# Low halves of split weights: a subtraction, or a negated copy and an accumulating DMA

## Chip, core and metric

One core of a Trainium2 chip runs the whole program. The metric is the time of one execution on the device in microseconds (us); the time of a kernel is the median of several runs. Profiles are of one execution each.

## What is computed

A trunk of two encoder layers on x of 512 tokens by 1024 features, all in float32. Cut to the lines that carry the large matrix products:

```python
def reference(x, ...):
    for l in range(DEPTH):                                   # DEPTH = 2
        h = x @ w_in[l]                                      # inside hybrid_mixer: 1024 -> 1824
        y_a = s5_mixer(...)                                  # state space scan and gated unit, 256 channels
        y_b = gla_mixer(...)                                 # gated linear attention, 4 heads, 256 channels
        y_c = swa_mixer(...)                                 # windowed attention, 8 heads, 512 channels
        mix = concatenate([y_a, y_b, y_c]) @ w_out[l]        # 1024 -> 1024
        x = layer_norm(DEEPNORM_ALPHA * x + mix, ln1_g[l], ln1_b[l])
        hid = square(relu(x @ w_ff1[l]))                     # 1024 -> 4096
        x = layer_norm(DEEPNORM_ALPHA * x + hid @ w_ff2[l], ln2_g[l], ln2_b[l])
    return x
```

## The kernel before

Every large product runs on TensorE (PE) in three passes. Both factors are split in a high half, the value copied to the type float32r, and a low half, the value minus that copy; `mm3` (lines 248 to 250) multiplies low by high, high by low and high by high into the same PSUM bank. The tensor `WA` holds six slots of such weight pairs, 128 x 2 x 1024 each, and the slots go round.

`wunit` (line 232) makes one unit, 128 rows by up to 1024 columns. SyncE (SP) issues the load of the float32 weights from HBM into one of two `raw` buffers (line 240), ScalarE (ACT) copies it to the high half (line 217, `copyA`), and VectorE (DVE) or GpSimd (POOL) subtracts the high half from raw to make the low half (line 244). Which engine subtracts is read from the table `CFG`: a letter for each of the four units of a matrix, G for POOL and V for DVE.

In each layer the input projection runs as four projections in the order g1, g0, g2, g3 (`proj`, 4 units each; g0 has units of 576 columns, the others of 1024), each over four token tiles of 128 with 24 matmuls a tile. The first twelve of a tile read x's feature tiles 0 to 3 and the units 0 and 1, the last twelve the feature tiles 4 to 7 and the units 2 and 3; in the trace the former read XTP and the latter XTQ in layer 0, XTQ and XTR in layer 1. Between the projections lie the S5 tables, states, scan and output, the GLA gates, scores, states and output, and four windowed softmax attention blocks. Then come w_out in two halves of 512 columns (keys wo0 and wo1, 4 units each), layer norm, the first four hidden tiles of w_ff1 (key f1e, 4 units), the rest of w_ff1 and w_ff2. The units of the rest of w_ff1 and of w_ff2 give `wunit` no engine and subtract on DVE; pairs of hidden tiles in seven products have a split of their own (line 1055).

With six slots, the third and fourth unit of a projection take the slots of the first two units of an earlier one. For g0, g2 and g3 this is the projection just before, so their copies wait until its last token tile has read those units.

The order on each engine's queue isn't the program's: a planner simulates the program with its own costs for instructions and DMAs as it writes the queues, and takes what is ready first. Each queue then runs in order on the chip and waits at semaphores. GpSimd's queue also holds the products of the GLA gates and keys, the softmax scaling of one head of each group of four (line 954), half of the table products of layer 0 and some additions of layer norm (line 226).

Of the kernel before, what the change touches and what calls it, by code (L numbers as in the profile page):

```python
# [13 lines left out]
AF = mybir.ActivationFunctionType  # L14
ALU = mybir.AluOpType
AX = mybir.AxisListType
MUL, ADD, SUB, MAX, MIN = ALU.mult, ALU.add, ALU.subtract, ALU.max, ALU.min

L = 512
D = 1024  # L20
# [7 lines left out]
CFG = {  # L28
    "ln": ["SA", "SA", "SA", "SA"],
    "ln2": ["A", "GV", "VG", "SS"],  # L30
    "lnl": ["AS", "SA", "S", "SS"],
    "f1e": "GGGV",
    "wo0": "GGGG",
    "wo1": "VVVV",
    "norm": "GVAV",
    "pt": "VAAV",
    "st": [12, 4],
# [15 lines left out]
    "gg": "GGGV",  # L53
    "sq": [["V", "A"], ["A", "A"]],
    "sa": "VVVV",
    "g0": "GGGG",
    "g1": "VVVG",
    "g2": "GVVV",
    "g3": "VVVV",
}  # L60
CONST_COLS = {"ident": 128, "tri_f": 128, "tri_b": 128, "tri_sf": 128, "tri_sb": 128,
              "rope_c": 64, "rope_s": 64, "pat": 16}
# [2 lines left out]
def trunk(tc, I, out, dbg=None):  # L65
    nc = tc.nc
# [134 lines left out]
        return t  # L201

    def yk(k):
        """(tile, index) of y's k-th row tile"""
        return (M.Ya, k) if k < 2 else (M.Yb, k - 2) if k < 4 else (M.Yc, k - 4)

    def bc(ap, axis, n):
# [5 lines left out]
    def act(o_, i_, f, **kw):  # L213
        S.activation(out=o_, in_=i_, func=f, **kw)  # L214
# [13 lines left out]
    state["pair"] = 0  # L228

    def E(k, i):  # L230
        return {"G": G, "V": V, "A": S}[CFG[k][i]]

    def wunit(src, eng=None, cuts=1):
        n = src.shape[-1]
        raw = rawp.tile([128, 1024], F32, tag="raw", name="raw")
        i = state["pair"] % 6
        state["pair"] += 1
        for j in range(cuts):
            c = slice(n * j // cuts, n * (j + 1) // cuts)
            nc.sync.dma_start(raw[:, c], src[:, c])  # L240
        for j in range(cuts):
            c = slice(n * j // cuts, n * (j + 1) // cuts)
            copyA(WA[:, i, 0, c], raw[:, c])
            (eng or V).tensor_tensor(WA[:, i, 1, c], raw[:, c], WAf[:, i, 0, c], op=SUB)  # L244
        return WA[:, i, 0, :n], WA[:, i, 1, :n]

    def mm3(ps, a, b, first, last):
# [35 lines left out]
        V.tensor_tensor(M.XS[i][:, :, 1], Tr[i], M.XSf[i][:, :, 0], op=SUB)  # L283

    def rsqrt(y, v, t):
        """y = v ** -0.5"""
        yi = y.bitcast(I32)
        V.tensor_scalar(yi, v.bitcast(I32), 1, None, op0=ALU.logical_shift_right)
        V.tensor_scalar(yi, yi, -1.0, float(0x5f3759df), op0=MUL, op1=ADD)
        for _ in range(3):  # L290
            V.tensor_tensor(t, y, y, op=MUL)
            V.scalar_tensor_tensor(t, t, -0.5, v, op0=MUL, op1=MUL)
            V.scalar_tensor_tensor(y, t, 1.5, y, op0=ADD, op1=MUL)
# [3 lines left out]
        nc.sync.dma_start(M.lnb, I[f"ln{which}_b"][l:l + 1, :].to_broadcast([128, 1024]))  # L297

    def layer_norm(tt, engs, nst=2, done=None):
        """engs: the engine that scales each of the tile's column parts"""  # L300
        x = XR[:, tt]
        s = LNS[:, tt]
        w = 1024 // nst
        for h in range(nst):
            V.bn_stats(s[:, 6 * h:6 * h + 6], x[:, w * h:w * h + w])
        mean, var, rstd, nmr, tmp = [s[:, i:i + 1] for i in (24, 25, 0, 1, 2)]
        V.bn_aggr(s[:, 24:26], s[:, 0:6 * nst].rearrange("p (a b) -> p a b", a=nst))
        n = 1024 // len(engs)
        parts = [(slice(n * h, n * h + n), e) for h, e in enumerate(engs)]
        early = [c for c, e in parts if e in "SA"]  # L310

        def centre():
            if early:
                c = early.pop(0)
                V.scalar_tensor_tensor(x[:, c], x[:, c], mean, M.lng[:, c], op0=SUB, op1=MUL)

        act(tmp, var, AF.Sqrt, bias=eps_c)
        V.tensor_scalar(var, var, EPS, None, op0=ADD)
        centre()
        V.reciprocal(nmr, tmp)  # L320
        centre()
        V.tensor_tensor(tmp, nmr, nmr, op=MUL)
        centre()
        V.scalar_tensor_tensor(tmp, tmp, -0.5, var, op0=MUL, op1=MUL)
        while early:
            centre()
        V.scalar_tensor_tensor(rstd, tmp, 1.5, nmr, op0=ADD, op1=MUL)
        if any(e not in "SA" for e in engs):
            V.scalar_tensor_tensor(nmr, mean, -1.0, rstd, op0=MUL, op1=MUL)
        for c, e in parts:  # L330
            if e == "S":
                V.scalar_tensor_tensor(x[:, c], x[:, c], rstd, M.lnb[:, c], op0=MUL, op1=ADD)
            elif e == "A":
                act(x[:, c], x[:, c], AF.Copy, scale=rstd)
                tt_(G, x[:, c], x[:, c], M.lnb[:, c], ADD)
            else:
                act(x[:, c], x[:, c], AF.Identity, scale=rstd, bias=nmr)
                tt_(G if e == "G" else V, x[:, c], x[:, c], M.lng[:, c], MUL)
                tt_(G if e == "G" and done else V, x[:, c], x[:, c], M.lnb[:, c], ADD)
            if done:  # L340
                done(c)
# [517 lines left out]
        copyA(M.gv[:, tt], ps[:, 256:512])  # L859

    def rope(x, n, tt):
        """x: [128, n, 64], its first 16 dims rotated in place"""
        c = bc(rope_c[:, tt], 1, n)
        s = bc(rope_s[:, tt].rearrange("p (a b) -> p a b", a=2), 1, n)
        t1 = RT[:, 0, 0:16 * n].rearrange("p (n d) -> p n d", n=n)
        t2 = RT[:, 1, 0:16 * n].rearrange("p (n a b) -> p n a b", n=n, a=2)
        r = x[:, :, 0:16]
        V.tensor_tensor(t1, r, c, op=MUL)
        V.tensor_tensor(t2, r.rearrange("p n (a b) -> p n a b", a=2)[:, :, ::-1], s, op=MUL)
        V.tensor_tensor(r, t1, t2.rearrange("p n a b -> p n (a b)"), op=ADD)  # L870
# [158 lines left out]
                xt(k, slice(t0, t1)), k == 0, k == 7)  # L1029

    def ff1_pair(l, i):
        """hidden row tiles i and i + 1 in seven products of halves (Winograd's form)"""
        q = state["st"] % 2
        state["st"] += 1
        r1, r2 = MA[:, 2048 * q:2048 * q + 1024], MA[:, 2048 * q + 1024:2048 * q + 2048]
        nc.sync.dma_start(r1, I["w_ff1"][l, i])
        nc.sync.dma_start(r2, I["w_ff1"][l, i + 1])
        s12 = rawp.tile([128, 1024], F32, tag="raw", name="s12")
        s1, s2, s4 = s12[:, 0:512], s12[:, 512:1024], MA[:, 6144:6656]
        tt_(E("sa", 0), s1, r2[:, 0:512], r2[:, 512:1024], ADD)  # L1040
        tt_(E("sa", 1), s2, s1, r1[:, 0:512], SUB)
        tt_(E("sa", 2), s4, r1[:, 512:1024], s2, SUB)
        tt_(E("sa", 3), r2[:, 0:512], r1[:, 0:512], r2[:, 0:512], SUB)

        def unit(src, half=None):
            if half != 1:
                u = state["pair"] % 6
                state["pair"] += 1
                if half == 0:
                    state["s4"] = u  # L1050
            else:
                u = state["s4"]
            c = slice(0, 1024) if half is None else slice(512 * half, 512 * half + 512)
            copyA(WA[:, u, 0, c], src)
            V.tensor_tensor(WA[:, u, 1, c], src, WAf[:, u, 0, c], op=SUB)  # L1055
            return WA[:, u, 0, c], WA[:, u, 1, c]

        wa, w12, w3 = unit(r1), unit(s12), unit(r2)
        w4 = unit(s4, q)
        pa, pb_ = psA("f1s"), psB("f1s")  # L1060
        pc = (psC, psE)[q]("f1s")
        p1, p5, p6, p7 = [pa[:, j // 2, 256 * (j % 2):256 * (j % 2) + 256] for j in range(4)]
        p2, p3, p4 = pb_[:, 0:256], pb_[:, 256:512], pc[:, 0:256]
        m1, u2, u3 = [MA[:, 4096 + 1024 * q + 256 * j:4352 + 1024 * q + 256 * j] for j in range(3)]
        r0, r1_ = ft_r[i % 2], ft_r[(i + 1) % 2]
        c12, c21, c22 = r0[:, 256:512], r1_[:, 0:256], r1_[:, 256:512]
        X1, X2 = M.XT
        T1, T2, T3, T4 = M.XS

        def prod(ps, w, c0, x):  # L1070
            for k in range(4):
                c = slice(c0 + 128 * k, c0 + 128 * k + 128)
                mm3(ps, (w[0][:, c], w[1][:, c]), (x[:, k, 0, 0:256], x[:, k, 1, 0:256]), k == 0, k == 3)

        prod(p1, wa, 0, X1)
        copyA(m1, p1)
        prod(p5, w12, 0, T1)
        prod(p6, w12, 512, T2)
        tt_(V, u2, m1, p6, ADD)
        tt_(V, c12, u2, p5, ADD)  # L1080
        prod(p7, w3, 0, T3)
        tt_(V, u3, u2, p7, ADD)
        tt_(V, c22, u3, p5, ADD)
        prod(p2, wa, 512, X2)
        tt_(V, r0[:, 0:256], m1, p2, ADD)
        prod(p3, w4, 0, X2[:, :, :, 256:512])
        tt_(V, c12, c12, p3, ADD)
        act(r0, r0, AF.Relu)
        ff_act(None, i)
        prod(p4, w3, 512, T4)  # L1090
        tt_(V, c21, u3, p4, SUB)
        act(r1_, r1_, AF.Relu)
        ff_act(None, i + 1)
# [40 lines left out]
                return  # L1134
            n = n and n - 1

# [1 line left out]
    nc.scalar.dma_start(cst["ident"], I["cst"][:, 0:128])  # L1138
    copyA(KON[:, 2:3], KON[:, 0:1])
    state["l"] = 0  # L1140
# [195 lines left out]
```

## Time and profile before

| | |
|---|---|
| median of 3 runs | 1257.71 us (1256.9 to 1258.25) |
| span of the profiled execution | 1254.5 us, 3.2 us below the median; no other time of it is recorded |
| PE busy | 1181.2 us, 94% of the span |
| PE weight loads busy | 982.9 us, 78% |
| DVE busy | 920.8 us, 73% |
| ACT busy | 551.0 us, 44% |
| POOL busy | 165.3 us, 13% |
| DMA moved | 119.60 MB, 95 GB/s on average |

The span runs from the first to the last instruction of the program. Busy time is the union of an engine's instructions; PE's matmuls overlap their weight loads. Of the span's 40 slices PE is busy less than 90% in eleven of the first and middle ones, where the mixers run, and nearly always in the feed-forward parts. POOL works in the first ten slices and again in the middle.

### The profile page before, as it was taken

Reading aid. Unit: us, or ns where it says so; the run is one execution under the profiler, and the core shown is the slowest. Engines: PE = TensorE matmul, PEld = TensorE weight load, DVE = VectorE, ACT = ScalarE, POOL = GpSimd, SP = SyncE. Lnnn points to the kernel's source line nnn. Section 1 sums busy time; section 2 is a strip of 40 time slices with the busy share of each in tenths; the row PEclk is TensorE's granted clock in tenths of the full one; section 3 lists DMA queues with packets and bytes.
Section 4 is the critical chain, followed back from the end, with each engine's and each line's share of the span. In section 5 each row is a group of like instructions: output and inputs, shape, how many; then the busy total and the mean of one; then the engine's idle time right before and its main releaser. Section 6 shows DMA issues by size and latency. Waiting matters only on the chain.

```text
span 1254.5 us, 18971 instructions
## 1 busy us (share of the span) xinstructions
PE 1181.2 (94%) x7400; PEld 982.9 (78%) x7400; DVE 920.8 (73%) x1918; ACT 551.0 (44%) x929; POOL 165.3 (13%) x123
## 2 busy tenths in 40 slices
PE   6798878999999999999999989799999999999997
PEld 4686555578888988989987857556898898998986
DVE  8995899969877765748564399883887575764857
ACT  3253247535521633615523634662464272561640
POOL 3423262112000000000041021220300000000000
PEclk9899989999999999999999999899999999999999
DMA  5440441113344422412422414202143242340331
GB/s 199 108 130 10 72 138 37 52 35 100 120 158 139 154 90 68 152 51 68 152 81 79 152 34 85 102 21 81 35 165 121 67 139 64 99 153 17 102 118 67
DMA packets 49610, 119.60 MB, mean 95 GB/s; under 512 B 13296, under 2 KB 20336, under 8 KB 49520
## 3 DMA queue, kind: packets, MB, share of 16 engines
q1 hardware_dynamic: 37680, 103.53, 25.5%
q10 hardware_dynamic: 11840, 14.86, 4.8%
q8 instruction: 58, 0.95, 0.3%
q14 instruction: 32, 0.26, 0.1%
HBM read 108.44 MB, written 8.88 MB: 94 GB/s over the span
## 4 chain that ended last, share of the span: by engine, by line
PE 78%; DVE 17%; DMA 2%; ACT 2%; issue 1%; SPq 0%; POOL 0%; DVEq 0%; ACTq 0%
PE o L248 11%; PE o L249 11%; PE o L250 11%; PE f1s L248 6%; PE f1s L250 6%; PE f1s L249 6%; PE proj L250 2%; PE proj L248 2%; PE proj L249 2%; PE so L963 2%; PE pT L957 1%; PE f L249 1%; PE f L250 1%; PE f L248 1%; PE f1e L249 1%
## 5 line engine op out<-in xcount | busy, mean ns | idle before, releaser
L217 ACT ACTIVATE WA<-raw 128x1024 fp32r<-128x1024 f32 (+2 forms) x129 | 132.7, 1029 | 152.2 <-PE o L250 43.1
L244 DVE TENSOR_TENSOR WA<-raw,WA 128x1024 fp32r<-128x1024 f32 (+1 forms) x102 | 122.2, 1198 | 86.1 <-ACT WA L217 86.0
L217 ACT ACTIVATE WA<-MA 128x1024 fp32r<-128x1024 f32 (+1 forms) x72 | 64.7, 914 | 146.9 <-PE o L250 106.4
L974 DVE SCALAR_TENSOR_TENSOR XR<-XR,o 128x512 f32<-128x512 f32 (+1 forms) x81 | 52.7, 675 | 100.8 <-PE o L250 100.6
L1055 DVE TENSOR_TENSOR WA<-MA,WA 128x1024 fp32r<-128x1024 f32 (+1 forms) x72 | 74.5, 1042 | 17.4 <-ACT WA L217 17.2
L248 PE MATMUL f1s<-xs,WA 128*128 128x256 f32 x288 | 81.4, 283 | 0.0
L249 PE MATMUL f1s<-xs,WA 128*128 128x256 f32 x288 | 81.2, 282 | 0.0
L250 PE MATMUL f1s<-xs,WA 128*128 128x256 f32 x288 | 80.9, 281 | 0.0
L244 POOL TENSOR_TENSOR WA<-raw,WA 128x1024 fp32r<-128x1024 f32 (+2 forms) x27 | 61.8, 2294 | 131.4 <-ACT WA L217 123.9
L226 DVE TENSOR_TENSOR MA<-MA,f1s 128x256 f32<-128x256 f32 x120 | 49.4, 417 | 32.7 <-PE f1s L250 20.9
L226 POOL TENSOR_TENSOR XR<-XR,lt 128x512 f32<-128x512 f32 (+1 forms) x13 | 18.4, 1418 | 398.3 <-ACT XR L214 398.3
L248 PE MATMUL o<-WA,yYa 128*128 128x512 f32 (+1 forms) x162 | 64.8, 400 | 0.8 <-DVE XR L974 0.7
L249 PE MATMUL o<-WA,yQ 128*128 128x512 f32 (+1 forms) x164 | 64.5, 393 | 0.0
L248 PE MATMUL o<-WA,yQ 128*128 128x512 f32 (+1 forms) x164 | 64.4, 392 | 0.0
L248 PE MATMUL o<-WA,yYb 128*128 128x512 f32 (+1 forms) x162 | 64.2, 396 | 0.0
L249 PE MATMUL o<-WA,yYb 128*128 128x512 f32 (+1 forms) x162 | 63.9, 395 | 0.0
L249 PE MATMUL o<-WA,yP 128*128 128x512 f32 x160 | 63.9, 399 | 0.0
L250 PE MATMUL o<-WA,yYa 128*128 128x512 f32 (+1 forms) x162 | 63.8, 394 | 0.0
L249 PE MATMUL o<-WA,yYa 128*128 128x512 f32 (+1 forms) x162 | 63.8, 394 | 0.0
L248 PE MATMUL o<-WA,yP 128*128 128x512 f32 x160 | 63.8, 399 | 0.0
L250 PE MATMUL o<-WA,yYb 128*128 128x512 f32 (+1 forms) x162 | 63.7, 394 | 0.0
L250 PE MATMUL o<-WA,yQ 128*128 128x512 f32 (+1 forms) x164 | 63.7, 391 | 0.0
(532 smaller groups left out, 3577.8 us busy)
## 6 DMA issues: line engine op xcount, KB each, us to landing
raw<-in_w_ff SPq DMA_DIRECT2D x80, 512.0 KB, 3.5
MA<-in_w_ff SPq DMA_DIRECT2D x48, 512.0 KB, 3.5
raw<-in_wg SPq DMA_DIRECT2D x23, 512.0 KB, 4.0
raw<-in_w_out SPq DMA_DIRECT2D x16, 512.0 KB, 3.8
scr_out<-MA SPq DMA_DIRECT2D x8, 512.0 KB, 4.2
yc<-scr_out ACTq DMA_DIRECT2D x8, 512.0 KB, 3.4
raw<-in_wg SPq DMA_DIRECT2D x8, 288.0 KB, 3.1
hx<-scr_lag ACTq DMA_DIRECT2D x16, 128.0 KB, 6.2
```

What stands on the lines that cost most here:

```text
L217: S.activation(out=o_, in_=i_, func=AF.Copy)
L226: eng.tensor_tensor(o_, a, b, op=op)
L244: (eng or V).tensor_tensor(WA[:, i, 1, c], raw[:, c], WAf[:, i, 0, c], op=SUB)
L248: T.matmul(ps, a[1], b[0], start=first, stop=False)
L249: T.matmul(ps, a[0], b[1], start=False, stop=False)
L250: T.matmul(ps, a[0], b[0], start=False, stop=last)
L957: T.transpose(ps[:, b * 128:b * 128 + 128], P[:, h, b * 128:b * 128 + 128], ident)
L963: T.matmul(ps[64 * v:64 * v + 64, :], av[:, tt - 1 + b0 + b, 64 * v:64 * v + 64], M.pT[v][:, b].rearrange("p h q -> p (h q)"), start=(b == ...
L974: V.scalar_tensor_tensor(x, x, scale, ps, op0=MUL, op1=ADD)
L1055: V.tensor_tensor(WA[:, u, 1, c], src, WAf[:, u, 0, c], op=SUB)
```

## The change

For units whose letter in `CFG` is D, `wunit` writes the negated high half into the low half's place with a second ScalarE copy, and a DMA issued from POOL reads the same weights from HBM again and adds them to it. `raw` is then read by the first copy alone. The letters of the four projections, of both halves of w_out and of w_ff1's first four units become D, except the first two units of the first projection: its first stays on POOL and its second moves from POOL to DVE. That is 26 units in each layer, 52 in all. The other edits take docstrings and a comment out.

```diff
-    "f1e": "GGGV",
-    "wo0": "GGGG",
-    "wo1": "VVVV",
+    "f1e": "DDDD",
+    "wo0": "DDDD",
+    "wo1": "DDDD",
...
-    "g0": "GGGG",
-    "g1": "VVVG",
-    "g2": "GVVV",
-    "g3": "VVVV",
+    "g0": "GVDD",
+    "g1": "DDDD",
+    "g2": "DDDD",
+    "g3": "DDDD",
...
     def E(k, i):
-        return {"G": G, "V": V, "A": S}[CFG[k][i]]
+        return {"G": G, "V": V, "A": S, "D": "D"}[CFG[k][i]]
...
             copyA(WA[:, i, 0, c], raw[:, c])
-            (eng or V).tensor_tensor(WA[:, i, 1, c], raw[:, c], WAf[:, i, 0, c], op=SUB)
+            if eng == "D":
+                act(WA[:, i, 1, c], WAf[:, i, 0, c], AF.Copy, scale=-1.0)
+                nc.gpsimd.dma_start(WA[:, i, 1, c], src[:, c], accum_op=ADD)
+            else:
+                (eng or V).tensor_tensor(WA[:, i, 1, c], raw[:, c], WAf[:, i, 0, c], op=SUB)
         return WA[:, i, 0, :n], WA[:, i, 1, :n]
```

The keys `g0` to `g3` of `CFG` stand for the projections in the order in which they run: `g0` for wg1, `g1` for wg0, `g2` for wg2 and `g3` for wg3.

## Rows read from the trace of the kernel before

**Rows 1.** The page: span, busy time and share of engines, chain that ended last.
```profile
span 1254.5 us, 18971 instructions
PE 1181.2 (94%) x7400; PEld 982.9 (78%) x7400; DVE 920.8 (73%) x1918; ACT 551.0 (44%) x929; POOL 165.3 (13%) x123
...
PE 78%; DVE 17%; DMA 2%; ACT 2%; issue 1%; SPq 0%; POOL 0%; DVEq 0%; ACTq 0%
```

**Rows 2.** Waits of PE: waiting group, what ended it, us in total, times, longest.
```profile
PE wst L564 <- DVE MA L554: 5.0, 1, 5.0
PE qT L902 <- DVE MA L465: 4.9, 1, 4.9
PE goT L707 <- POOL ya L226: 4.6, 2, 3.7
...
PE sy L814 <- DVE GLS L288: 3.1, 2, 2.5
...
PE xt L257 <- DVE XTR L262: 2.0, 1, 2.0
PE f1e L249 <- DVE XTR L262: 1.7, 1, 1.7
```

**Rows 3.** Instructions on the tile raw: ns min/median/max, first to last start, shapes.
```profile
L244 DVE TENSOR_TENSOR WA<-raw,WA x102: 743/1224/1637, 30.5 to 1216.9; 128x1024 fp32r<-128x1024 f32 x96, 128x576 fp32r<-128x576 f32 x6
...
L244 POOL TENSOR_TENSOR WA<-raw,WA x27: 1262/2392/2837, 5.6 to 892.5; 128x1024 fp32r<-128x1024 f32 x23, 128x512 fp32r<-128x512 f32 x2, 128x576 fp32r<-128x576 f32 x2
```

**Rows 4.** Timeline, POOL and DVE, layer 0: start us, us, engine, line, operation.
```profile
21.70 4.75 POOL L244 TENSOR_TENSOR WA<-raw,WA 128x1024 fp32r<-128x1024 f32 x2 [8.28 <-ACT WA L217]
...
174.09 4.66 POOL L244 TENSOR_TENSOR WA<-raw,WA 128x1024 fp32r<-128x1024 f32 x2 [2.09 <-issue]
...
176.51 2.27 DVE L288 TENSOR_SCALAR GLS<-GLS 128x8 int32<-128x8 int32 x1
178.81 0.17 DVE L289 TENSOR_SCALAR GLS<-GLS 128x8 int32<-128x8 int32 x1
```

**Rows 5.** Timeline of DVE: five of the twenty instructions beside POOL subtractions.
```profile
5.66 1.26 DVE L432 SCALAR_TENSOR_TENSOR KD<-KD 128x16 f32<-128x16 f32 x1
...
21.87 2.27 DVE L456 TENSOR_TENSOR KD<-KD 128x16 f32<-128x16 f32 x1
...
656.39 2.36 DVE L324 SCALAR_TENSOR_TENSOR LNS<-LNS 128x1 f32<-128x1 f32 x1
...
783.22 2.35 DVE L292 SCALAR_TENSOR_TENSOR GLS<-GLS 128x8 f32<-128x8 f32 x1
...
893.26 2.10 DVE L322 TENSOR_TENSOR LNS<-LNS 128x1 f32<-128x1 f32 x1
```

**Rows 6.** Timeline, layer 0, third unit of g3: copy, subtraction, first two matmuls.
```profile
125.15 1.06 ACT L217 ACTIVATE WA<-raw 128x1024 fp32r<-128x1024 f32 x1 [2.21 <-PE proj L250]
...
128.62 1.23 DVE L244 TENSOR_TENSOR WA<-raw,WA 128x1024 fp32r<-128x1024 f32 x1
...
130.05 0.39 PE L248 MATMUL proj<-WA,XTQ 128*128 128x512 f32 x1
...
130.28 0.40 PE L249 MATMUL proj<-WA,XTQ 128*128 128x512 f32 x1
```

**Rows 7.** Timeline, layer 1, third unit of g0: copy, first matmul.
```profile
682.16 0.69 ACT L217 ACTIVATE WA<-raw 128x576 fp32r<-128x576 f32 x1 [2.39 <-PE proj L250]
...
686.12 0.30 PE L248 MATMUL proj<-WA,XTR 128*128 128x288 f32 x1
```

**Rows 8.** DMA issues of raw: count, KB each, median us to landing; minimum, median, maximum.
```profile
raw<-in_wg SPq DMA_DIRECT2D x23, 512.0 KB, 4.0
...
raw<-in_wg SPq DMA_DIRECT2D x8, 288.0 KB, 3.1
...
DMA to landing us min/median/max: 2.6/3.5/6.9
```

## The prediction

> **What bounds the kernel now.** I read the page's engine totals and the chain that ended last first [rows 1]. TensorE (PE) is busy for 1181.2 of 1254.5 us, so no more than 73.3 us of the span are free of matrix work, and the chain lies 78% on PE and 17% on VectorE (DVE). A faster DVE can gain only where PE waits for it. The second view is therefore PE's waits [rows 2]: the six listed sum to 21.3 us. They end on DVE work or on what follows directly from it, in the two stretches before w_ff1, where tables, scan, gates, softmax and layer norm run between the matmuls. From 300 us on in layer 0 and 920 us in layer 1 nothing changes but the first four w_ff1 units before it.
>
> The third view is the instructions on the raw weight tile [rows 3]: the subtractions of line 244 are 102 on DVE, median 1.22 us, and 27 on GpSimd (POOL), median 2.39. The fourth is the timeline of DVE and POOL side by side [rows 4]. While POOL ran two subtractions from 174.09 for 4.66 us, DVE's 128x8 operation at 176.51 took 2.27 us, and a like one at 178.81, after POOL had ended, 0.17. So a POOL subtraction costs DVE nearly its own length. Going through DVE's timeline I count twenty instructions that lasted at least 1 us longer than their like while POOL subtracted; the first and the last are shown, with three between them [rows 5]. Their excess adds up to 34 us.
>
> **What the change removes.** Per layer 12 units of 1024 columns and 3 of 576 leave DVE, and one (the second unit of the first projection) comes to it from POOL: 12 x 1.22 + 3 x 0.74 - 1.22 = 15.6 us (the median and, for the narrow ones, the shortest of [rows 3]), 31 us in two layers. 24 of POOL's 27 subtractions go, and with them all but some 2 us of the 34 us of stalls, since the two at the very start stay. That is 63 us of DVE time, yet each piece is worth only the PE wait behind it:
> - Tables of layer 0: PE waited 5.0 us for DVE before "wst" [rows 2]. Two POOL subtractions took 4.75 us from 21.70 [rows 4], in which the DVE chain got two short operations done, the first of them 2.27 us long [rows 5]: 4.3 us freed, and further subtractions of the same stretch free over 1 us. Gain 5.0, capped by the wait.
> - End of the projections of layer 0: "qT" waited 4.9 us [rows 2]; before it lie 4.66 us under POOL [rows 4] and two subtractions of 1.23 on DVE [rows 6]. Gain 4.9, capped.
> - Start of layer 1: a transpose of x waited 2.0 us [rows 2] after a layer norm operation of 2.36 us at 656.39 [rows 5]. Gain 2.0.
> - GLA output of layer 1: "goT" and "sy" waited 4.6 and 3.1 us in both layers [rows 2]; the operation at 783.22 took 2.35 us [rows 5] where 0.16 is usual. Gain 2.2.
> - First w_ff1 matmuls of layer 1: 1.7 us of waiting [rows 2] behind the 2.10 us at 893.26 [rows 5]. Gain 1.7.
>
> Together 15.8 us. What is late next at each place is PE itself. For the subtractions outside these places, on POOL or DVE, I count nothing: the DVE time that they free lies beside PE work.
>
> **What the change adds.** Each of the 52 units gets a second ScalarE (ACT) copy like the first, 1.06 us for 1024 columns [rows 6] and 0.69 for 576 [rows 7], 52 us in all, and a DMA issued from POOL that reads the weight again and adds it into WA. ACT holds 2% of the chain [rows 1], so nearly all of its 52 us lie beside other work; the bounds are 0 and, if the eight w_out copies that fall among the softmax's exponentials, four in each layer, each delay one by a whole copy, 8.5 us. I take 1.5, near the lower end, because of that 2%.
>
> The accumulating DMA is not in this trace. Its lower bound is the plain load of as many bytes; its upper bound the slowest such load, 6.9 us, plus one POOL operation of the size that it replaces, 2.3 us, for making the request: 9.2. In between: 512 KB land in 4.0 us and 288 KB in 3.1 [rows 8], so 224 KB cost 0.9 us, 512 KB 2.1 and the fixed part is 1.9. If the bytes pass twice (source and old contents) this gives 1.9 + 2 x 2.1 = 6.1 us, and 4.3 for 288 KB. I take this estimate; the lower end is the fastest plain median, 4.0.
>
> So the low half comes 1.06 + 6.1 = 7.2 us after the high half, where DVE's subtraction took 1.2. Most units have more room, their slots being free long before they are read. Not so the third and fourth unit of a projection, since their slot comes free only near the end of the projection before. In layer 0 the copy starts at 125.15, the subtraction at 128.62, and PE reads the unit first at 130.05, the thirteenth matmul of the XTQ run [rows 6]: 4.9 us of room for 2 x 1.06 + 6.1 = 8.2 us, short by 3.3. For a 576-column unit, copied at 682.16 and read at 686.12 [rows 7]: 4.0 us for 2 x 0.69 + 4.3 = 5.7, short by 1.7. There are eight such places, six wide and two narrow: 23 us if PE merely waited. But the planner that orders the queues can put the next token tile's twelve matmuls on the units already there in between: 12 x 0.23 = 2.8 us by the step from 130.05 to 130.28 [rows 6], and 1.6 for 288 columns. That leaves 6 x 0.5 + 2 x 0.1 = 3.2 us. I take 6.0: cover everywhere but at one wide place.
>
> On POOL the DMA waits for the second copy, and behind it wait the GLA products, the softmax scalings and layer norm's additions. A subtraction there waited for the first copy and held POOL for 2.3 us, so 24 places get no worse unless the request costs more than that; at the 28 places that were DVE's the added hold is up to 2.3 us, on an engine with little to do. SP's loads are not passed by anything; a raw buffer even comes free at the first copy instead of at the subtraction, which is worth nothing where the copy waits for a slot.
>
> **The sum.** 1254.5 - 15.8 + 6.0 + 1.5 = 1246.2 us of span. The median of the runs is 1257.71, 3.2 us above this span; with the same 3.2 the forecast is 1249.4, so 1249.
>
> The Trainium skill ("DMA: Bandwidth & Descriptors", section on the anatomy of one DMA) fits a GpSimd-issued DMA with 2.0 us plus bytes/436e3, an estimate of 3.2 us for 512 KB. The trace's loads of that size, issued from SP, take 4.0. By the page's figure the narrow places would have room and the wide ones would lack 0.4 us, which the reordering covers; the late units would cost next to nothing and the time would be about 1243.
>
> **Rivals.**
> 1. The low halves come late (slower). Mechanism: at the eight tight places PE stands at the first matmul of the third unit. For it speaks that the rooms of 4.9 and 4.0 us are real, against it that the planner can cover 2.8 us of each. At a DMA of 9.2 us the wide places lack 11.3 - 4.9 - 2.8 = 3.6 us even with cover, the narrow ones about as much: 29 us, so 1257.7 - 15.8 + 29 + 1.5 = 1272. It turns the sign once these places cost 14.3 us together, that is from a DMA of 7.5 us with all covers (3.2 + 8 x 1.4) and of 5.0 without any (23 - 8 x 1.1).
> 2. POOL's requests are held up by DVE (no change). They use what the subtractions used: [rows 4] show one of the two engines standing while the other works. If each request at a tight place waits for one long DVE instruction, 1.2 us as in [rows 6], 8 x 1.2 = 9.6 us are added: 1259. Against it: DVE's instructions in the tables and norms are mostly 0.2 to 0.7 us. The skill's page "SBUF — State Buffer", section "Who interferes with whom", gives this as a rule that speaks against the change: descriptor generation for a DMA issued from GpSimd is starved while DVE holds the shared port pair. No row here has such a DMA.
> 3. The freed DVE time is hidden (no change or nearly). Other POOL work, such as the table products and the softmax scalings, stays and still stalls DVE, and PE's order is rearranged; if half of the 15.8 us is lost, 1257.
> 4. More than I count: waits too small for my list close too, and all covers hold: 1257.7 - 20 = 1238.
>
> **How the numbers follow.** Forecast (1242 to 1255) 0.56; more gain (below 1242) 0.11; rivals 2 and 3 together 0.13; rival 1 0.20. The two ends of the DMA's cost give 1244 (at 4.0 us a wide place lacks 1.2, taken once) and 1272; the range 1235 to 1264 leaves out some 0.15 above and 0.04 below. 0.2% is 2.5 us, about what a measurement of this kernel can tell from no change. Faster 0.67, same 0.13, slower 0.20.
>
> **What would show each step.** Right: the 2 us operations on DVE among ones of 0.17 are gone but for the first units; line 244 on DVE falls by some 30 us, POOL by 50; "wst", "qT" and the layer norm waits shrink; ACT is busy some 52 us more. Wrong: PE waits named after WA's DMA at the third unit of projections, with sums above 10 us; landings over 7 us; POOL's requests of 2 us or more. What would overturn it altogether is a DMA that needs over 9 us from request to landing.

## The result and the profile after

| | before | after |
|---|---|---|
| median of the runs, us | 1257.9 | 1300.7 |
| profiled execution, span, us | 1254.5 | 1298.6 |
| ratio of times, 95% interval | | 1.0348 [1.0335, 1.0361] |
| PE busy, us | 1181.2 | 1196.7 |
| DVE busy, us | 920.8 | 865.2 |
| ACT busy, us | 551.0 | 597.2 |
| POOL busy, us | 165.3 | 149.6 |

The changed kernel is 3.5% slower; the prediction was 1249, faster. Its page, with the lines that answer to [rows 1] (span, busy time by engine, chain that ended last):

```profile
span 1298.6 us, 19069 instructions
...
PE 1196.7 (92%) x7400; PEld 992.2 (76%) x7400; DVE 865.2 (67%) x1890; ACT 597.2 (46%) x981; POOL 149.6 (12%) x151
...
PE 71%; DVE 12%; DMA 9%; issue 4%; ACT 2%; SPq 0%; POOL 0%; ACTq 0%; DVEq 0%; POOLq 0%
```

DVE is 56 us less busy, as intended, and its share of the chain falls from 17 to 12%. But DMA rises from 2 to 9%. POOL is only 16 us less busy, since 52 requests come where 24 subtractions go. PE does the same 7400 matmuls and is busy 15.5 us longer; with that goes a lower mean granted clock, 0.964 in the profiled run after and 0.982 in the one before (f3 and f4 below show the two together). The waits of PE, as in [rows 2] (waiting group, what ended it, us in total, times, longest):

```profile
PE proj L253 <- DMA WA<-in_wg: 17.6, 7, 5.6
PE sy L820 <- DMA yc<-scr_out: 11.0, 4, 6.4
PE wst L568 <- DVE MA L558: 9.8, 1, 9.8
PE f1e L252 <- DMA WA<-in_w_ff: 6.2, 2, 3.8
...
PE sv L743 <- DMA TAB<-scr_st: 4.5, 1, 4.5
```

Two kinds of wait are new. The first and fourth line are low halves that come late, 23.8 us. The second and the last end on DMAs that the change never touched. The third, "wst", was 5.0 us before and should have gone away; it doubled. The DMA issues of the page after (count, KB each, median us from issue to landing):

```profile
raw<-in_wg SPq DMA_DIRECT2D x23, 512.0 KB, 6.0
WA<-in_wg POOLq DMA_DIRECT2D x20, 512.0 KB, 8.5
...
WA<-in_w_out POOLq DMA_DIRECT2D x16, 512.0 KB, 6.6
...
WA<-in_w_ff POOLq DMA_DIRECT2D x8, 512.0 KB, 7.6
raw<-in_wg SPq DMA_DIRECT2D x8, 288.0 KB, 5.2
WA<-in_wg POOLq DMA_DIRECT2D x8, 288.0 KB, 8.3
```

The accumulating DMAs land in 6.6 to 8.5 us, and the plain loads beside them, 4.0 and 3.1 us in [rows 8], now take 6.0 and 5.2.

How "wst" came to double can be read from DVE's waits in the first 62 us and POOL's timeline (start us, us, engine, line, operation, idle before):

```profile
DVE CI L1167 <- DMA RT<-in_ci: 7.7, 1, 7.7
```

```profile
51.88 1.26 POOL L558 TENSOR_TENSOR MA<-lt 128x512 f32<-128x512 f32 x1
53.09 0.88 POOL L246 DMA_DIRECT2D WA<-in_wg  x1
53.70 1.35 POOL L559 TENSOR_TENSOR lt<-MB,TAB 128x512 f32<-128x512 f32 x1
54.71 1.35 POOL L560 TENSOR_TENSOR lt<-MB,TAB 128x512 f32<-128x512 f32 x1
55.71 1.19 POOL L246 DMA_DIRECT2D WA<-in_wg  x1
```

DVE, which makes the tables of layer 0, stood 7.7 us for a load of constants. Behind it the tables came later, and POOL's products of the tables with them, and the two requests for g0's third and fourth unit, ready when their second copies ended at 44.4 and 45.8, stood behind those products until 53.1 and 55.7. The subtractions they replace were on DVE and in no such queue.

### The profile page after: what moved, and what is told of

Same layout as the page of the kernel before. It is cut to its first block, busy times and chain, and to the rows that moved or that the text cites. A ratio compares the mean times of both kernels' runs of the same rounds, so it can differ in the third digit from the quotient of the medians.

```text
span 1298.6 us, 19069 instructions
## 1 busy us (share of the span) xinstructions
PE 1196.7 (92%) x7400; PEld 992.2 (76%) x7400; DVE 865.2 (67%) x1890; ACT 597.2 (46%) x981; POOL 149.6 (12%) x151
## 4 chain that ended last, share of the span: by engine, by line
PE 71%; DVE 12%; DMA 9%; issue 4%; ACT 2%; SPq 0%; POOL 0%; ACTq 0%; DVEq 0%; POOLq 0%
PE o L252 11%; PE o L253 11%; PE o L254 11%; PE f1s L252 6%; PE f1s L253 6%; PE f1s L254 6%; DMA yc<-scr_out 2%; DMA WA<-in_wg 2%; PE so L967 2%; PE f1e L252 1%; PE f1e L254 1%; PE f1e L253 1%; PE f L254 1%; PE f L253 1%; PE f L252 1%
## 5 line engine op out<-in xcount | busy, mean ns | idle before, releaser
L248 DVE TENSOR_TENSOR WA<-raw,WA 128x1024 fp32r<-128x1024 f32 x74 | 90.5, 1223 | 56.4 <-ACT WA L217 56.2
L253 PE MATMUL o<-WA,yP 128*128 128x512 f32 x160 | 63.7, 398 | 0.0
L252 PE MATMUL o<-WA,yP 128*128 128x512 f32 x160 | 63.5, 398 | 0.0
L254 PE MATMUL o<-WA,yP 128*128 128x512 f32 x160 | 63.4, 398 | 0.0
```

Of the source, the lines that this page charges most:

```text
L252: T.matmul(ps, a[1], b[0], start=first, stop=False)
L253: T.matmul(ps, a[0], b[1], start=False, stop=False)
L254: T.matmul(ps, a[0], b[0], start=False, stop=last)
```

## The experiments

Two theories stood at the start. A: the accumulating DMA is slow and shares the DMA engines with all other loads. B: the order of the queues, which the planner makes anew for each kernel, and the second ACT copies eat the gain.

### Four runs in the planner's own order

e1_plain: the DMA without its accumulation (the low half becomes the whole weight), every queue in the order of the changed kernel.

```diff
-                nc.gpsimd.dma_start(WA[:, i, 1, c], src[:, c], accum_op=ADD)
+                nc.gpsimd.dma_start(WA[:, i, 1, c], src[:, c])
```

> The changed kernel with the accumulation taken out of the DMA: it writes the weight itself into the low half, so the output lacks the correction that the low half stands for. Every engine's queue has the same order as in the changed kernel. Theory A (the accumulating DMA is slow and delays PE and other loads): its packets take 159 ns instead of 328, landings fall from a median of 7.4 us to about 5, and the time falls by 15 us or more, to 1285 or less. Theory B (the planner's new order and the second ScalarE copies cost the time, whatever the DMA takes): within 5 us of 1300.

Measured: 1275.6 us, 1.0142 [1.0119, 1.0165], as theory A had it. In the traces PE has its matmuls in the same order as in the changed kernel; there the accumulation alone costs 25 us.

e2_no_dma: no DMA at all (the low half stays minus the high half).

```diff
-                nc.gpsimd.dma_start(WA[:, i, 1, c], src[:, c], accum_op=ADD)
```

> The changed kernel without the accumulating DMAs: the low half stays the negated high half, so the correction by the low half is wrong in these 52 units. The second copies stay, the subtractions are gone. Theory A: about 1243 (1257.7 minus the 15.8 us of waits counted in the prediction, plus 1.5 for the copies), in any case below 1252. Theory B: above 1258, since the copies and a rearranged order remain.

Measured: 1261.4 us, 1.0039 [1.0028, 1.0051], as theory B had it. Without a single late low half nothing is gained over the kernel before. So the DMA alone doesn't explain the miss: 15.8 us of gain were missing here too.

e3_projections and e4_wout_ff1: the change for the projections alone, and for w_out and w_ff1 alone.

```diff
-    "f1e": "DDDD",
-    "wo0": "DDDD",
-    "wo1": "DDDD",
+    "f1e": "GGGV",
+    "wo0": "GGGG",
+    "wo1": "VVVV",
```

> Only the projections' units use the copy and the DMA (28 of 52); w_out and the first w_ff1 units subtract as before. Theory A: nearly the whole loss, 1285 to 1300, since the units without room are all here. Theory B: the loss in proportion, 28 of 52, about 1281.

```diff
-    "g0": "GVDD",
-    "g1": "DDDD",
-    "g2": "DDDD",
-    "g3": "DDDD",
+    "g0": "GGGG",
+    "g1": "VVVG",
+    "g2": "GVVV",
+    "g3": "VVVV",
```

> Only w_out and the first w_ff1 units use the copy and the DMA (24 of 52); the projections subtract as before. Theory A: no loss, 1248 to 1258, since these units have room and the layer norms and the GLA output no longer stall beside POOL. Theory B: the loss in proportion, 24 of 52, about 1278.

Measured: 1294.8 us, 1.0299 [1.0274, 1.0324], and 1265.1 us, 1.0067 [1.0047, 1.0087]. The first is what theory A had, the second lies between the two. Most of the loss belongs to the projections, where the tight units are. But every one of these kernels also has an order of its own, so no difference between them except that of e1 is clean.

### The order of before, imposed

From here on the order is held fixed. The kernel carries, for each instruction in the order of tracing, its place in the built kernel before, and ties each instruction to the one ahead of it on its engine by an edge that orders but doesn't wait (cut from the function that does it):

```diff
+    last = {}
+    for k in order:
+        if k not in base:
+            continue
+        for i in extra[k] if base[k] is None else [base[k]] + extra.get(base[k].name, []):
+            e = str(i.engine)
+            if e in last:
+                tc.add_manual_dep(i, last[e].name, mybir.DependencyInfo(
+                    mybir.DependencyClass.NoSync, mybir.DependencyReason.DATA), reason="order")
+            last[e] = i
```

`extra` holds what replaces a subtraction: the second copy right behind the first, and the request on POOL at that same point. For four w_out units, whose slots hold attention data until late, it stands where the subtraction stood. The second unit of either layer stays with POOL as before. In the traces of f1 to f9 the 7400 matmuls of PE stand in the order of before. The kernel before with its own order imposed was not run, so what imposing it does by itself is not shown.

f1_free_order_kept: the 52 subtractions are dropped, nothing replaces them.

```diff
-    "g0": "GVDD",
+    "g0": "GGDD",
...
-                act(WA[:, i, 1, c], WAf[:, i, 0, c], AF.Copy, scale=-1.0)
-                nc.gpsimd.dma_start(WA[:, i, 1, c], src[:, c], accum_op=ADD)
+                DROPS.append((nc.cur_bb.bb.instructions[-1].name, 0))
+                pass
...
-        return WA[:, i, 0, :n], WA[:, i, 1, :n]
+        return WA[:, i, 0, :n], WA[:, i, 0 if eng == "D" else 1, :n]
```

`DROPS` notes the first copy and how many instructions behind it are new, for the order; the edits below leave that line out.

> Every engine has its instructions in the order of the kernel before; the 52 subtractions are gone and nothing stands in their place: the matmuls read the high half twice, so the low halves are left out of the result. Theory A (the 15.8 us of freed VectorE waits are real, and what ate them in the run without DMA was the new order of the queues and the second copies): 1257.7 - 15.8 = 1242 us, 1238 to 1246. Theory B (the freed VectorE time is hidden, TensorE's waits only change their name): 1252 to 1257 us. Theory C (the order of before fits only its own durations, so keeping it loses something): above 1257 us.

Measured: 1233.0 us, 0.9804 [0.9780, 0.9827], below what any of the three had. Dropping the subtractions is worth 25 us, not 15.8, and the freed DVE time is not hidden. A little of the 25 is something else: f1 reads no low half in these units, so the one listed wait of PE for one of their low halves in before, 2.4 us, is gone too.

f2_copies_order_kept: f1 with the second ACT copies.

```diff
-                pass
+                act(WA[:, i, 1, c], WAf[:, i, 0, c], AF.Copy, scale=-1.0)
```

> The same order, and a second, negated ScalarE copy behind each first one, still without DMA: the low half is minus the high one, so the result lacks the weights. Theory A (ScalarE's copies lie beside other work): 1 to 3 us above the run without copies, so about 1244 us. Theory B (the copies, not the order, ate the gain of the run without DMA at 1261 us): 12 us or more above the run without copies, 1254 to 1262 us. The difference from that run of 1261 us is the price of the new order.

Measured: 1242.7 us, 0.9880 [0.9854, 0.9906]. The copies cost 10 us, which neither theory named: too much for A, too little for B. The same work in the planner's order, but for the second unit, was e2, 1261.4: that order costs some 19 us.

f3_accumulate_order_kept: f2 with the DMAs, that is the whole change in the order of before.

```diff
+                nc.gpsimd.dma_start(WA[:, i, 1, c], src[:, c], accum_op=ADD)
```

> The same order, second copies and accumulating DMAs as in the changed kernel, except that the second unit of all stays on GpSimd. Theory A (the DMA costs what it cost in the changed kernel, the order is a separate loss): plain against accumulating differed by 25 us and plain against none by 14 at the planner's own order, so 1244 + 39 = 1283 us, 1275 to 1290. Theory B (the planner's order was chosen to cover late low halves, so without it TensorE stands at every third unit): 8 places at some 5 us more, 1300 us or above. Theory C (the loss is mostly the order): below 1265 us.

Measured: 1304.4 us, 1.0355 [1.0312, 1.0399]. As theory B had it, the DMAs cost more, 62 us, in an order that doesn't make room for them. Its waits of PE (as above):

```profile
PE proj L254 <- DMA WA<-in_wg: 33.5, 13, 5.5
PE sy L821 <- DMA yc<-scr_out: 10.4, 3, 6.4
```

There are thirteen waits for low halves in the projections instead of the seven of the changed kernel: there the planner's order covered about half of them. The place of [rows 6], the third unit of layer 0's g3, in the timeline of PE and of POOL in f3:

```profile
136.84 0.39 PE L255 MATMUL proj<-WA,XTQ 128*128 128x512 f32 x1
137.07 0.40 PE L253 MATMUL proj<-WA,XTQ 128*128 128x512 f32 x1
142.39 0.80 PE L254 MATMUL proj<-WA,XTQ 128*128 128x512 f32 x1 [4.92 <-DMA WA<-in_wg]
142.99 0.63 PE L255 MATMUL proj<-WA,XTQ 128*128 128x512 f32 x1
143.41 0.63 PE L253 MATMUL proj<-WA,XTQ 128*128 128x512 f32 x1
```

```profile
134.63 0.87 POOL L247 DMA_DIRECT2D WA<-in_wg  x1 [3.13 <-ACT WA L214]
```

The request starts 0.3 us after the second copy and PE goes on 7.8 us after it. Only the second of a unit's three matmuls needs the low half of the weight, so the first, at 137.07, could run and the next stood 4.92 us. After that stand the matmuls follow each other in 0.42 us instead of 0.23. The table by stretches of f3, just before and just after it (from:to, us, busy of PE, PEld, DVE, ACT, POOL with counts, granted clock, share of the DMA engines, GB/s):

```profile
133.40:137.40 4.00, 4.00 (x22) 3.14 (x20) 3.90 (x11) 3.97 (x6) 1.60 (x2) 1.00 0.67 156
142.40:145.40 3.00, 2.92 (x6) 1.82 (x6) 1.42 (x5) 0.00 (x0) 1.72 (x1) 0.50 0.95 189
```

The granted clock was 1.00 until the stand and 0.50 behind it, 1.2 instead of 2.4 GHz, and the DMA engines are 95% busy.

f4_traffic_nobody_waits: f3, but the matmuls read the high half twice, so no one waits for what the DMAs write.

```diff
-        return WA[:, i, 0, :n], WA[:, i, 1, :n]
+        return WA[:, i, 0, :n], WA[:, i, 0 if eng == "D" else 1, :n]
```

> The kernel with accumulating DMAs in the order of before (1304 us), but the matmuls of those 52 units read the high half twice, so nobody reads what the DMAs write, and the low halves are left out of the result. Same requests, same bytes, same copies; no matmul can wait for them. Theory A (late low halves are the loss): the 34 us of matmul waits on WA's DMA go, and with them what the granted clock lost behind them (TensorE is busy 25 us longer than in the run with copies alone): 1250 to 1262 us. Theory B (the traffic is the loss: it slows the other loads, and requests hold GpSimd): 1285 us or above.

Measured: 1273.3 us, 1.0113 [1.0084, 1.0142], between the two theories: both are half right. Late low halves cost 1304.4 - 1273.3 = 31 us. The DMAs alone, traffic and requests on POOL, with nobody waiting for what they write, cost 1273.3 - 1242.7 = 31 us (the matmuls of f2 do read the second copies, but none of its listed waits ends on one). A row of the same table for f3 and one for f4, over g1 of layer 0 and what runs beside it:

```profile
11.80:48.40 36.60, 31.43 (x120) 24.18 (x121) 26.16 (x122) 14.82 (x24) 12.58 (x12) 0.91 0.64 169
```

```profile
13.90:43.40 29.50, 27.73 (x120) 22.14 (x121) 21.20 (x106) 14.66 (x24) 7.80 (x8) 1.00 0.70 180
```

The same 120 matmuls take 31.43 us of PE in f3 and 27.73 in f4, at a granted clock of 0.91 and 1.00, that is with and without some time at the lower of its two levels. Over the whole run PE is busy 1201.4 us in f3 and 1184.0 in f4: of the 31 us that late low halves cost, 17 are not waiting but matmuls that took longer, at a mean granted clock of 0.963 instead of 0.973. The 33.5 us of waits on WA's DMA count in part only, since behind them other waits shrink ("wst", 7.9 us in f4, is 1.8 in f3).

Where these 31 us lie is read from f2 against f4: DVE's waits in the first 62 us, first f2, then f4,

```profile
DVE CI L1167 <- DMA RT<-in_ci: 1.5, 1, 1.5
```

```profile
DVE CI L1168 <- DMA RT<-in_ci: 6.0, 1, 6.0
```

PE's waits in f4,

```profile
PE sy L821 <- DMA yc<-scr_out: 9.6, 3, 5.2
PE wst L569 <- DVE MA L559: 7.9, 1, 7.9
PE qT L907 <- DVE MA L647: 7.7, 1, 7.7
...
PE uT L728 <- DMA yc<-yb: 5.1, 1, 5.1
...
PE sv L744 <- DMA TAB<-scr_st: 3.7, 1, 3.7
```

and the landings in f4:

```profile
raw<-in_wg SPq DMA_DIRECT2D x23, 512.0 KB, 6.3
...
yc<-scr_out ACTq DMA_DIRECT2D x8, 512.0 KB, 8.1
```

In f2 the same two loads take 3.6 and 5.3 us, "wst" waits 4.1 us, "qT" behind line 646 3.8, "sy" 1.3 and "uT" 2.0. The matmuls wait for loads and for DVE work that itself waited for a load: ahead of "qT", DVE stands 7.4 us for the load of GLG, 3.5 in f2. No wait of PE that ends on POOL is longer ("goT", 0.9 us in both). PE is also busy 8 us longer, 1184.0 instead of 1176.0.

f8_traffic_plain: f4 with plain DMAs.

```diff
-                nc.gpsimd.dma_start(WA[:, i, 1, c], src[:, c], accum_op=ADD)
+                nc.gpsimd.dma_start(WA[:, i, 1, c], src[:, c])
```

> As the run in which nobody reads what the DMAs write (1273 us; order of before, low halves left out of the result), but the DMAs don't accumulate: same requests from GpSimd, same order, same source bytes, no old contents read. Theory A (the second pass of the bytes slows the other loads): half of the 31 us of traffic goes or more, 1250 to 1259 us, and the loads of the projections land in some 4.5 us instead of 6.3. Theory B (the requests on GpSimd and the waits ahead of them are the price): 1266 to 1274 us, with GpSimd's products as late as before.

Measured: 1256.8 us, 0.9986 [0.9970, 1.0002]. As theory A had it, 16.5 of the 31 us are gone, with as many requests: raw lands in 4.6 us, the DMAs into WA in 6.0 instead of 8.8, and the wait for RT's load is 3.8 us instead of 6.0. So accumulating is a little over half of the price of the DMAs. It isn't the bytes alone that changed, since a plain request takes 0.53 us on POOL and an accumulating one 0.87. The other 14 us are the plain bytes or the requests on POOL; these two were not separated.

### Kernels that could be better

f5_dma_where_room and f6_dma_where_most_room: the order of before, DMAs only for the 36 units that had room in f3, and for the 20 with the most. The first edit is against f3, the second against f5.

```diff
-    "g0": "GGDD",
-    "g1": "DDDD",
-    "g2": "DDDD",
-    "g3": "DDDD",
+    "g0": "GGGG",
+    "g1": "DDVG",
+    "g2": "DDVV",
+    "g3": "DDVV",
```

> The order of before; DMAs only for 36 units whose low half landed at least 3.8 us ahead of its first matmul in the run with all of them: units 0 and 1 of the second to fourth projection, all of w_out and the first w_ff1. The third and fourth unit of each projection keep their subtraction. Theory A (late low halves are the loss): no matmul waits for WA's DMA, most of the gain of 25 us stays, copies cost 36/52 of 10 us and the rest of the traffic some 5: 1245 to 1253 us, faster than before. Theory B (traffic): 36/52 of 62 us on top of 1243, 1275 us or above.

```diff
-    "f1e": "DDDD",
+    "f1e": "GGGV",
...
-    "wo1": "DDDD",
+    "wo1": "VVVV",
```

> The same with DMAs for 20 units only: units 0 and 1 of the second to fourth projection and the first half of w_out, the ones with the most room; w_out's second half and the first w_ff1 keep their subtractions. Theory A: fewer copies and less traffic against a smaller gain, 1246 to 1255 us. Theory B: 20/52 of 62 us on top of 1248, 1265 us or above.

Measured: 1270.8 us, 1.0095 [1.0065, 1.0124], and 1265.9 us, 1.0066 [1.0046, 1.0087]. A miss of theory A: f5 lies between the two theories, f6 where B had it. Also where the low half has room the change loses against before. In f5 two waits of the first w_ff1 matmuls for a late low half, 3.5 us together, have a part in it. In f6 none of PE's waits that the view lists ends on WA's DMA, and the longest in sum is this one, 1.3 us in f2:

```profile
PE sy L821 <- DMA yc<-scr_out: 10.5, 3, 6.5
```

f7_gpsimd_to_dve: no DMA; POOL's subtractions run on DVE, order kept. The edit is against the kernel before.

```diff
-    "f1e": "GGGV",
-    "wo0": "GGGG",
+    "f1e": "VVVV",
+    "wo0": "VVVV",
...
-    "g0": "GGGG",
-    "g1": "VVVG",
-    "g2": "GVVV",
+    "g0": "GGVV",
+    "g1": "VVVV",
+    "g2": "VVVV",
```

> The order of before and no DMA: 24 of GpSimd's 27 subtractions run on VectorE instead, at the same place; nothing is left out. Theory A (a GpSimd subtraction costs VectorE nearly its own length, as the prediction had it): 34 us of stalls go, 24 x 1.22 = 29 us of subtractions come, so the time changes by little: 1250 to 1258 us. Theory B (the two share less than that, the stalls were something else): 15 to 25 us more, 1272 us or above.

Measured: 1247.2 us, 0.9914 [0.9897, 0.9930]: faster than both kernels, and a little faster than either theory had it. It moves 22 subtractions, not the 24 of the text above, since the first two units of layer 1 stay on POOL as well. The page of f7:

```profile
span 1244.2 us, 18965 instructions
...
PE 1179.3 (95%) x7400; PEld 982.4 (79%) x7400; DVE 914.8 (74%) x1940; ACT 552.0 (44%) x929; POOL 114.0 (9%) x101
```

DVE has 22 instructions more and is busy 6.0 us less than before. So 22 x 1.22 = 27 us of added subtractions replace some 33 us of stalls: here a POOL subtraction costs DVE some 1.5 us, more than the 1.22 of doing it itself.

f9_gpsimd_to_dve_all moves the remaining five too.

```diff
-    "g0": "GGVV",
+    "g0": "VVVV",
```

> The order of before, no DMA, all 27 of GpSimd's subtractions on VectorE (the 24 of the earlier run, 1247 us, and the three of the first two units, before the first projection); nothing is left out. Theory A (each GpSimd subtraction stalls VectorE): at the start VectorE has only the first transposes to split, so 0 to 2 us less, 1245 to 1247 us. Theory B (at the start VectorE is the chain itself and GpSimd a help): 1 to 3 us more, 1248 to 1250 us.

Measured: 1246.4 us, 0.9909 [0.9894, 0.9925], the same as f7.

f10_gpsimd_to_dve_own_order: f7 in the planner's own order.

```diff
-        freeze(tc, nc.cur_bb, DROPS)
```

> The same 24 subtractions moved from GpSimd to VectorE, but every queue in the order that the planner makes of it by itself. Theory A (the planner's new order costs as much as in the run without DMA, 1261 us against 1243 in the order of before): some 15 us above the run in the order of before, 1257 to 1265 us. Theory B (that loss belongs to the units with DMAs or second copies): 1245 to 1250 us.

Measured: 1283.4 us, 1.0205 [1.0186, 1.0224]. The same instructions as f7 take 36 us longer, more than either theory had. PE's waits of f10:

```profile
PE sc L928 <- ACT MA L214: 8.8, 4, 3.8
PE gsc L641 <- ACT MA L217: 8.6, 3, 3.8
PE sy L814 <- DMA hx<-scr_lag: 6.6, 1, 6.6
PE proj L248 <- DVE XTP L262: 5.0, 1, 5.0
PE uT L723 <- DMA yc<-yb: 4.6, 1, 4.6
```

They are spread over attention scores, gates, scan and projections, and none of these ends on a moved subtraction. Since the instructions are those of f7, the order is the loss; 10 of the 36 us are a PE busy longer, 1189.6 us instead of 1179.3. Why the planner's order of this kernel is worse was not tried.

## Why the prediction was wrong

The step that failed is the price of the DMAs. The prediction had 6.0 us for late low halves and nothing for what the added transfers do to others; the runs show 31 and 31.

| step | predicted, us | measured, us | from |
|---|---|---|---|
| 52 subtractions gone | -15.8 | -25 | before to f1 |
| second copies | +1.5 | +10 | f1 to f2 |
| DMAs that nobody waits for | 0 | +31 | f2 to f4 |
| low halves late | +6.0 | +31 | f4 to f3 |
| planner's order instead of that of before | 0 | -4 | f3 to after |

The measured sum is +43, from 1258 to 1301. Each step is the difference of two medians and good to some 4 to 7 us; the last is within its own uncertainty. It also depends on where it is taken: without DMAs the planner's order cost 19 us (f2 to e2).

- What bounds the kernel: right. PE waits for DVE in the places that [rows 2] list, and dropping the subtractions is worth more than the prediction's 15.8 us, 25. By stage, between before and f1, the projections of layer 0 got 9.5 us shorter (tables: 5.0 predicted), the way from there to w_out 4.6 (4.9 predicted), the start of layer 1 1.9 (2.0), its GLA and attention 4.4 (2.2), its first w_ff1 1.7 (1.7). Part of it is faster matmuls: PE is busy 6 us less in f1, 1175.2 us. The rest is waits too small for the list. That stalls beside POOL go: right, f7 shows it apart.
- The copies: 1.5 us predicted, 10 measured, above the upper bound of 8.5, by less than the two runs can tell. The bound thought only of exponentials; f2 loses 3.5 us in the projections of layer 1 and the rest in small pieces. The 2% of ACT in the chain of before was no ground for the lower end.
- The DMA itself: the term that was mis-sized, 6.1 us predicted for 512 KB in the projections and 8.5 measured, 4.3 and 8.3 for 288 KB. That the bytes pass twice fits: a packet of 4096 bytes takes 328 ns (median) on POOL's queue in the changed kernel and 174 on the same queue where the DMA doesn't accumulate (f8). But plain and unread they still land in 6.0 us in f8, where the prediction started from 4.0 for a load issued by SP. Whether that is the other loads beside them or the issue from POOL is not shown. With 8.5 and 8.3 the prediction's own formula gives 2 x 1.06 + 8.5 - 4.9 = 5.7 us at a wide place and 1.4 + 8.3 - 4.0 = 5.7 at a narrow one, 46 us for eight without cover and 26 with it. After shows 17.6 us in seven waits, f3, without the planner's cover, 33.5 in thirteen.
- By the fit of the Trainium skill ("DMA: Bandwidth & Descriptors", section "Anatomy of one DMA") the landing of 512 KB would have been 3.2 us, an estimate, and the time 1243; the accumulating DMAs of that size, with other loads beside them, took 6.6 to 8.5. The prediction's remark that the narrow places then have room is off by 0.1 us, which changes nothing.
- Missing altogether: what 25.4 MB more do to the loads of other queues. The prediction said that SP's loads are not passed by anything, and counted nothing; between f2 and f4 the loads of raw go from 3.6 to 6.3 us and those of yc on ACT's queue from 5.3 to 8.1. The whole step is 31 us, as much as the late low halves; how much of it is the requests on POOL was not separated. That f5 and f6 lose by the same is likely, since "sy" waits as long there as in f4, but was not tried apart.
- Missing too: what PE loses after a wait. The prediction counted a late low half at its waiting time; f3 against f4 shows 17 us of longer matmuls on top.
- The cover by the planner: half right. It halves the waits for low halves, yet the new order loses elsewhere what it wins: f3 and after are 4 us apart.
- POOL: a request takes 0.86 us, below the 2.3 feared, and they aren't held up by DVE (median 0.86, longest 1.20 us). The Trainium skill ("SBUF — State Buffer", section "Who interferes with whom") has descriptor generation starved while DVE holds the shared port pair; these times show no such delay, and no run tells when DVE held the pair. What did bite is the queue ahead of a request, 8.7 and 9.9 us at g0's third and fourth unit.
- The rivals: the first, low halves late, is what happened, though its 1272 had neither the traffic nor the clock. Of the third, that the freed DVE time is hidden is refuted by f1; that a rearranged order loses the gain is what e2 shows, 19 us above f2. The fourth, more gain than counted, holds for the subtractions alone.

## What to carry to other kernels

Here an added transfer was paid three times: by its reader when it was late, by the loads of other queues beside it, and by matmuls that ran at the lower clock after a stand. Ask for each stretch which loads are tight there before adding bytes to it. A subtraction on GpSimd that stalls VectorE for longer than VectorE would need for it is better on VectorE, at a fixed order (f7). And where a planner orders the queues, compare kernels at a fixed order: here the order alone moved the time by 19 and 36 us, while the largest gain of any run that leaves nothing out was 11.

## What the runs showed of the hardware

- On POOL's queue a packet of 4096 bytes takes 328 ns (median) when the DMA accumulates and 174 when it doesn't; 512 KB land in 8.8 and 6.0 us, and the request takes 0.87 and 0.53 us on POOL (f4, f8).
- A load of 128 KB on another queue, RT<-in_ci, lands in 3.6 us in f2, 5.7 with plain and 7.8 with accumulating DMAs beside it (f8, f4).
- After 4.9 us without a matmul PE went on at a granted clock of 0.50, the lower of its two levels (1.2 GHz), 0.42 us a matmul instead of 0.23 (f3).
- 22 float32 subtractions of 128 rows moved from POOL to DVE made DVE 6.0 us less busy in all (f7).
